# Dense token chunks ranked one by one beside the gate stage, with TensorE's order written out there

## The chip, the cores and the metric

One core of a Trainium2 chip runs the kernel. TensorE (PE; its weight loads are PEld), VectorE (DVE), ScalarE (ACT), GpSimd (POOL) and SyncE (SP, which here issues most transfers) work side by side, each through its own list in order, and wait for each other by semaphores. The metric is the device time of one execution in microseconds; the median of three runs of the kernel before is 1878.28 us (1877.82 to 1882.6).

## What is computed

One layer of a decoder on 512 prompt tokens and 64 sample tokens. Two branches (a short convolution, and attention over a window of 128 with sinks) are merged by sigmoid gates, normed, and followed by a product-key expert layer, which takes most of the time:

```python
qv = einsum('nd,de->ne', xb, w_pq)                      # 8 heads, two halves of 128
s = einsum('nhpc,hpkc->nhpk', qv, sub_keys)             # 128 keys in each half
top_s, top_i = lax.top_k(s, 16)                         # the 16 best of each half
best_s, sel = lax.top_k(sums_of_pairs(top_s), 16)       # the 16 best pairs = experts
gate = softmax(best_s)
pre = einsum('nd,nhkd->nhk', xb, expert_u[idx])         # 16384 experts
out = einsum('nhk,nhkd->nd', gate * gelu(pre), expert_v[idx])
y = layer_norm(alpha * h + out)
```

`sums_of_pairs` stands here for the sums of the two halves' best keys, with the expert's number beside each.

## The kernel before

**Waves and chunks.** Tokens go through in two waves. The first wave holds chunk 0 and the sample chunk; their experts' rows are gathered one by one (an indirect DMA on GpSimd, a multiply-and-sum on VectorE: tile `junk`, line 525). The second wave holds the dense chunks 1, 2 and 3 (128, 128 and 64 tokens; the sixty-four rows beside chunk 3 come from the first wave). For these all 16384 experts are computed, in 128 tables of 128 experts, and a gate matrix with zeros picks the chosen ones.

**Float32 by halves.** A matrix product of float32 numbers is three matmuls: each operand is split into a high part (`whi`, on ScalarE, line 119) and the rest (`wlo`, on GpSimd or VectorE, line 120), and `mm3` (lines 123 to 125) adds three of the four products.

**The second wave's stages.**
- Projections, convolution, and attention, which needs the mask `mask_p`, the keys `kT_all` and the values `v_all`.
- The merge of the convolution branch (`merge_conv`): eight times a gate product of 24 matmuls and a convolution product of 12, multiplied on VectorE into the tile `br` (line 661). The convolution products lie in one of three PSUM banks, which `br`'s multiply frees. The merge of the attention branch follows, then the output projection, the norm and the transposes.
- Key scores (`scores`): sixteen weight tables, four per call. After each call VectorE ranks each chunk's 4 heads' halves (`top16`, five instructions for a list of 128) and, when a group of heads has both halves, `route` forms and ranks the pairs and turns them into key numbers.
- First products (`front`): table t of `expert_u` times the tokens, 24 matmuls of 384 columns, GELU, result to DRAM (`spill`) for the first 60 tables and kept for 9 more: 69 (`AHEAD`) in all before the second product begins.
- The gate stage (`gate_matrix`): per four tokens one VectorE comparison makes two one-hot matrices (`hot`, line 785), ScalarE and GpSimd scale one of them by the gate weights, four matmuls (eight instructions in the trace) multiply them, ScalarE or VectorE copies the result into `gb`, and every sixteen tokens `gb` goes to DRAM (`gd`). Three `hot` buffers and three PSUM banks serve it.
- The second product: for each of 128 tables, GELU times gate (`gm`, read back from `gd`), split, 18 matmuls into six banks (`acc`, line 937), and, from the 61st table on, one more first product beside it.

**What sets the order.** The program is recorded in the order of the code; a scheduler that simulates a timeline then puts each engine's instructions in order, and `issue_after` pins one behind another. Gathers of the first wave are woven in as `side` work, one to two after each table. In the code before, five first products follow each call of `scores`, all three chunks are ranked there, and during the gate stage first products are released by a proportion, ten (`KEEP`) being held back and pinned behind the last gate matmul:

```python
for k, g4 in enumerate((0, 2, 1, 3)):
    scores(second, g4)
    fronts(FQ * (k + 1))
...
for i in range(len(DENSE)):
    for g in gate_matrix(i, *second.sel[i], gd):
        fronts(base + (AHEAD - KEEP - base) * (i * (128 // GN) + g + 1) // total)
with tc.issue_after(newest[1]):
    fronts(AHEAD)
```

Of the kernel before, what the change touches and what calls it, by code (L numbers as in the profile page):

```python
# [17 lines left out]
AF = mybir.ActivationFunctionType  # L18
# [41 lines left out]


ORDER = "qkscscasacsca"
FQ = 5
KEEP = 10
LAST = 2


# [8 lines left out]
def step_kernel(ctx: ExitStack, tc: tile.TileContext, I: dict, O: dict):  # L76
# [28 lines left out]
    loads, newest = [], [None, None]  # L105

    def late(dst, src):

# [13 lines left out]
    def mm3(ps, L, R, start, stop):  # L122
        PE.matmul(ps, L[0], R[0], start=start, stop=False)  # L123
        PE.matmul(ps, L[0], R[1], start=False, stop=False)  # L124
        PE.matmul(ps, L[1], R[0], start=False, stop=stop)  # L125

    def in_order(calls):
        last = None
# [22 lines left out]
    side_work = []  # L151

    def side(n):
        while n > 0 and side_work:
            try:
                next(side_work[0])
                n -= 1
            except StopIteration:
                side_work.pop(0)
# [261 lines left out]
    def route(val, pos, sel, hs):  # L421
# [36 lines left out]
        for k, (s1, s2, off) in enumerate((((4, ALU.logical_shift_right), (2, ALU.logical_shift_right), -12.0),  # L458
                                           ((15, ALU.bitwise_and), (3, ALU.bitwise_and), 0.0))):
            u1 = f128("u1", U32)  # L460
            u2 = f128("u2", U32)
            V.tensor_single_scalar(u1, bp, s1[0], op=s1[1])
            V.tensor_single_scalar(u2, bp, s2[0], op=s2[1])
            rk = f128("rk")
            V.scalar_tensor_tensor(rk, u2, off, u1, op0=ALU.add, op1=ALU.subtract)
            V.tensor_tensor(rk, rk, mk, op=ALU.mult)
            V.tensor_tensor(rk, rk, u1, op=ALU.add)
            oh = tmp("k", [128, 4, 16, 16], "oh", dt=BF16)[:r]
            V.tensor_tensor(oh.rearrange("p h k a -> p (h k) a"), rk.unsqueeze(2).broadcast_to([r, 64, 16]),
                            numbers[0][:r, :16].unsqueeze(1).broadcast_to([r, 64, 16]), op=ALU.is_equal)  # L470
            V.tensor_tensor(oh, oh, pf[:, :, k, :].unsqueeze(2).broadcast_to([r, 4, 16, 16]), op=ALU.mult)
            V.tensor_reduce(keys[k], oh.rearrange("p h k a -> p (h k) a"), axis=AX.X, op=ALU.add)

    def key_tiles():
        return [tmp("k", [128, 128], f"kk{k}", bufs=3) for k in range(2)]
# [187 lines left out]
    def merge_attention(s):  # L663
# [59 lines left out]
        if s.w == 0:  # L723
# [4 lines left out]
        s.sel = [sel3 if c == 3 else (key_tiles(), gate[c] if c in GATHER else tmp("k", [128, 128], "gt", bufs=2))  # L728
                 for c in s.chunks]

    def scores(s, g4):

        sk = tmp("w", [128, 512], "raw", name="sk", bufs=RAW["w"])
        S.dma_start(sk, I["sub_keys"][g4])
        low = g4 < 2
        pss = []
        for i, r in enumerate(s.rows):
            if r == 128:
                pss.append(bank("mm"))
            else:  # L740

                if low:
                    s.half = bank("mm")
                pss.append(s.half[:64] if low else s.half[64:128])
        for j in range(4):
            ps = product(s, weight(s, I["w_pq"][g4 * 4 + j]), s.hT, 8, "u")
            qv = tmp("k", [128, s.mv], "qv", bufs=2)
            A.activation(qv, ps, AF.Copy)
            for i, r in enumerate(s.rows):
                where = dict(tile_position=(0, 64)) if r == 64 and not low else {}  # L750
                PE.matmul(pss[i][:, j * 128:(j + 1) * 128], qv[:, i * 128:i * 128 + r],
                          sk[:, j * 128:(j + 1) * 128], start=True, stop=True, **where)
        for i, r in enumerate(s.rows):
            if r == 64 and low:
                continue
# [3 lines left out]
            for j in range(4):  # L759
                top16(s.val[i][:, g * 4 + j, :], s.pos[i][:, g * 4 + j, :], sc[:, j, :], 128)  # L760
            if r == 64 and g == 1:
                keys, gt = s.sel[i]
                kh, gh = [tmp("k", [128, 64], f"kh{k}") for k in range(2)], tmp("k", [128, 64], "gh")
                route(s.val[i], s.pos[i], (kh, gh), 0)
                for dst, src in zip((*keys, gt), (*kh, gh)):
                    A.activation(dst[:64, :64], src[:64], AF.Copy)
                    S.dma_start(dst[:64, 64:128], src[64:128])
            elif r == 128 and g4 % 2:
                route(s.val[i], s.pos[i], s.sel[i], g4 // 2)


    def gate_matrix(i, keys, gt, gd):
# [3 lines left out]
        iota_ps = pt[:, 384:512]  # L776
        T = tmp("k", [128, 3, 128], "T3")
        A.activation(T, pt[:, :384].rearrange("p (k n) -> p k n", k=3), AF.Copy)
        for g in range(128 // GN):
            gb = tmp("b", [128, 128, GN], "gb", bufs=2)  # L780
            for q in range(GN // 4):
# [5 lines left out]
                for r in range(4):  # L787
                    oi = hot[:, 0, r, :]
                    weight_of = T[:, 2, n + r:n + r + 1]
                    if GATED[r] == "a":  # L790
                        A.activation(oi, oi, AF.Copy, scale=weight_of)  # L791
                    else:
                        G.tensor_scalar(oi, oi, weight_of, None, op0=ALU.mult)
                    newest[1] = PE.matmul(ps[:, r * 128:(r + 1) * 128], hot[:, 1, r, :], oi, start=True, stop=True).ins  # L794
# [6 lines left out]
            S.dma_start(gd[i * (128 // GN) + g], gb)  # L801
            yield g


    spill = dram.tile([NS, 128, ND], F32, name="spill")
# [2 lines left out]
    ks, bs = ExitStack(), ExitStack()  # L808
    pools["k"] = ks.enter_context(pool("k", "left"))
    pools["mm"] = ks.enter_context(psum("mm", 3))  # L810
    at_stack = ExitStack()
    pools["at"] = at_stack.enter_context(psum("at", 3))
    sel3 = ([tmp("k", [128, 128], f"k3{k}") for k in range(2)], tmp("k", [128, 128], "gt3"))
# [36 lines left out]
    hT = second.hT  # L850
    coef = {}

    def front(t):
        wu = table(I["euT"][t], "w", G if t < AHEAD else V, PACE_U[t % len(PACE_U)] if t < AHEAD else 0)
        ps = bank("u")
        for k in range(8):
            mm3(ps[:, :ND], block(wu, k), (hT[0][:, k, :], hT[1][:, k, :]), k == 0, k == 7)
# [9 lines left out]
    done = 0  # L867

    def fronts(n):
        nonlocal done  # L870
        while done < min(n, NE):
            front(done)
            done += 1

    for k, g4 in enumerate((0, 2, 1, 3)):
        scores(second, g4)
        fronts(FQ * (k + 1))
    total = len(DENSE) * 128 // GN
    base = done
    for i in range(len(DENSE)):  # L880
        for g in gate_matrix(i, *second.sel[i], gd):
            fronts(base + (AHEAD - KEEP - base) * (i * (128 // GN) + g + 1) // total)
    with tc.issue_after(newest[1]):
        fronts(AHEAD)
    bs.close()
    ks.close()
    del pools["hp"]
# [39 lines left out]
        return calls  # L927

    for t in range(NE + 1):
        fronts(t + LAG)  # L930
        if t < NE:
            middle(t)
        if 1 <= t <= NE - LAST:
# [115 lines left out]
```

## Time and profile before

| | us |
|---|---|
| median of the runs | 1878.28 |
| profiled execution, its own time | 1882.06 |
| its span | 1880.3 |
| TensorE busy | 1733.5 (92%) |
| VectorE busy | 1507.2 (80%) |
| GpSimd busy | 1111.2 (59%) |
| ScalarE busy | 782.1 (42%) |
| DMA, mean rate | 264 GB/s |

Times in rows count from the span's start. A busy TensorE is not TensorE at its peak: its matmuls overlap, so what counts is the distance from one start to the next. PEclk is the granted clock: 1.00 is its higher level (2.4 GHz), 0.5 its lower (1.2 GHz), and a value between is a mix of both over the stretch. An engine's idle time costs only where another waits for it. In the page's chain that ended last TensorE holds 49%, VectorE 24%, transfers 10%.

### The profile page before, as it was taken

To read this page: it belongs to the slowest core of one execution; us is meant where nothing else is said; L and a number is where in the kernel's file an instruction comes from. 1 tells how busy PE (TensorE), PEld (TensorE's weight loads), DVE (VectorE), ACT (ScalarE), POOL (GpSimd) and SP (SyncE) were. 2 spreads that over 40 slices of the span, in tenths; PEclk is the share of its full clock that TensorE was granted. 3 is DMA by queue.
4 is the path that set the end of the run, shared out by engine and by line. 5 is a ranking of instruction groups with operands and counts; after the bars stand their busy time and mean duration, and the time that the engine had idled before them with its cause. 6 is when DMAs were issued, how large, how long until landed. Compare 5 with 4: busy or idle time off the path is not lost.

```text
span 1880.3 us, 27617 instructions
## 1 busy us (share of the span) xinstructions
PE 1733.5 (92%) x9760; PEld 1573.5 (84%) x9760; DVE 1507.2 (80%) x2632; ACT 782.1 (42%) x1339; POOL 1111.2 (59%) x724
## 2 busy tenths in 40 slices
PE   7999998897989998699979899999999999999985
PEld 7997798887779888699978777787899999998974
DVE  6646689998955699998896677878778888888897
ACT  4554343442333433367785333333333333343322
POOL 4445433466756667688835522223578777778883
PEclk9999999997989999799999899999999999999998
DMA  7445443357757678799947999999989999989973
GB/s 246 156 134 213 130 135 118 113 186 254 277 192 249 232 239 276 248 326 363 338 187 253 330 327 328 345 336 341 322 311 353 335 327 353 350 299 339 326 264 108
DMA packets 190539, 496.50 MB, mean 264 GB/s; under 512 B 17712, under 2 KB 83696, under 8 KB 187312
## 3 DMA queue, kind: packets, MB, share of 16 engines
q1 hardware_dynamic: 135104, 293.39, 45.5%
q0 software_dynamic: 55296, 201.35, 30.1%
q8 instruction: 76, 1.25, 0.3%
q14 instruction: 63, 0.52, 0.1%
HBM read 454.48 MB, written 40.54 MB: 263 GB/s over the span
## 4 chain that ended last, share of the span: by engine, by line
PE 49%; DVE 24%; DMA 10%; issue 7%; POOL 5%; ACT 5%; SPq 1%; DVEq 0%; POOLq 0%; ACTq 0%
PE acc L937 19%; PE ps L123 9%; PE ps L124 8%; PE ps L125 8%; POOL wlo L120 3%; DMA re<-spill 3%; DVE junk L525 3%; PE ps L794 2%; POOL g L511 2%; DVE wlo L120 2%; DMA raw<-in_euT 2%; ACT whi L119 1%; ACT hot L791 1%; DMA g<-in_eu,idx 1%; DVE s L415 1%
## 5 line engine op out<-in xcount | busy, mean ns | idle before, releaser
L120 POOL TENSOR_TENSOR wlo<-raw,whi 128x1024 fp32r<-128x1024 f32 x232 | 580.0, 2503 | 320.6 <-ACT whi L119 287.9
L119 ACT ACTIVATE whi<-raw 128x1024 fp32r<-128x1024 f32 x388 | 409.2, 1056 | 590.0 <-PE ps L124 235.9
L123 PE MATMUL ps<-xhi,whi 128*128 128x384 f32 (+2 forms) x1600 | 531.3, 332 | 34.3 <-ACT sp L860 27.8
L125 PE MATMUL ps<-xhi,wlo 128*128 128x384 f32 (+2 forms) x1600 | 527.4, 330 | 1.6 <-POOL wlo L120 1.6
L124 PE MATMUL ps<-xlo,whi 128*128 128x384 f32 (+2 forms) x1600 | 527.6, 330 | 0.0
L534 DVE SCALAR_TENSOR_TENSOR h<-g,pre,h 128x1024 f32<-128x1024 f32 x192 | 316.2, 1647 | 71.7 <-DMA g<-in_ev,idx 70.4
L511 POOL DMA_INDIRECT g<-in_eu,idx x192 | 206.6, 1076 | 241.3 <-DVE junk L525 186.5
L123 PEld LDWEIGHTS ps<-xhi,whi 128*128 128x128 f32 x1600 | 309.6, 194 | 44.3 <-ACT sp L860 30.3
L511 POOL DMA_INDIRECT g<-in_ev,idx x192 | 255.0, 1328 | 126.5 <-DVE h L534 87.3
L124 PEld LDWEIGHTS ps<-xlo,whi 128*128 128x128 f32 x1600 | 309.3, 193 | 3.6 <-issue 0.9
L125 PEld LDWEIGHTS ps<-xhi,wlo 128*128 128x128 f32 x1600 | 308.6, 193 | 3.0 <-POOL wlo L120 2.1
L937 PE MATMUL acc<-whi,chi 128*128 128x512 f32 x756 | 292.4, 393 | 14.7 <-ACT chi L119 8.4
L937 PE MATMUL acc<-wlo,chi 128*128 128x512 f32 x756 | 299.6, 396 | 5.7 <-POOL wlo L120 5.7
L937 PE MATMUL acc<-whi,clo 128*128 128x512 f32 x756 | 258.1, 394 | 2.1 <-DVE clo L120 2.1
L120 DVE TENSOR_TENSOR wlo<-raw,whi 128x1024 fp32r<-128x1024 f32 x156 | 204.6, 1312 | 49.1 <-ACT whi L119 48.9
L937 PEld LDWEIGHTS acc<-whi,chi 128*128 128x128 f32 x756 | 143.1, 189 | 47.1 <-ACT chi L119 11.7
L937 PEld LDWEIGHTS acc<-wlo,chi 128*128 128x128 f32 x756 | 144.1, 191 | 37.0 <-POOL wlo L120 8.2
L525 DVE SCALAR_TENSOR_TENSOR junk<-g,hp 128x1024 bf16<-128x1024 f32 x104 | 125.7, 1209 | 56.9 <-DMA g<-in_eu,idx 54.8
L937 PEld LDWEIGHTS acc<-whi,clo 128*128 128x128 f32 x756 | 143.6, 190 | 32.8 <-DVE clo L120 2.7
L785 DVE TENSOR_TENSOR hot<-pt,T 128x1024 f32<-128x1024 f32 x96 | 114.0, 1217 | 17.1 <-PE ps L794 12.1
L525 DVE SCALAR_TENSOR_TENSOR junk<-g,h 128x1024 bf16<-128x1024 f32 x88 | 123.7, 1406 | 3.1 <-DMA g<-in_eu,idx 2.8
L794 PE MATMUL ps<-hot 128*128 128x128 f32 x768 | 111.6, 289 | 15.2 <-ACT hot L791 14.0
(252 smaller groups left out, 2205.5 us busy)
## 6 DMA issues: line engine op xcount, KB each, us to landing
raw<-in_euT SPq DMA_DIRECT2D x128, 512.0 KB, 6.1
raw<-in_ev SPq DMA_DIRECT2D x128, 512.0 KB, 5.0
gd<-gb SPq DMA_DIRECT2D x24, 1024.0 KB, 5.2
gm<-gd SPq DMA_DIRECT2D x48, 512.0 KB, 9.7
raw<-in_w_g SPq DMA_DIRECT2D x32, 512.0 KB, 3.4
raw<-in_w_pq SPq DMA_DIRECT2D x32, 512.0 KB, 4.2
raw<-in_w_bch SPq DMA_DIRECT2D x24, 512.0 KB, 3.5
spill<-sp SPq DMA_DIRECT2D x60, 192.0 KB, 4.2
```

Source lines behind the costliest of these rows:

```text
L119: A.activation(hi, src, AF.Copy)
L120: return (eng or V).tensor_tensor(lo, src, hi.bitcast(F32), op=ALU.subtract)
L123: PE.matmul(ps, L[0], R[0], start=start, stop=False)
L124: PE.matmul(ps, L[0], R[1], start=False, stop=False)
L125: PE.matmul(ps, L[1], R[0], start=False, stop=stop)
L415: V.match_replace(s2, val[:, 0:8], s, -3.0e38)
L511: G.indirect_dma_start(out=rows[i], out_offset=None, in_=I[src], in_offset=bass.IndirectOffsetOnAxis(ap=idx[c][:, s:s + 1], axis=0))
L525: V.scalar_tensor_tensor(junk, g, 1.0, in_psum(c), op0=ALU.mult, op1=ALU.mult, accum_out=p)
L534: V.scalar_tensor_tensor(h_tok[c], g, p, h_tok[c], op0=ALU.mult, op1=ALU.add)
L785: V.tensor_tensor(hot, iota_ps.unsqueeze(1).unsqueeze(1).broadcast_to([128, 2, 4, 128]), T[:, 0:2, n:n + 4].unsqueeze(3).broadcast_to([128 ...
L794: newest[1] = PE.matmul(ps[:, r * 128:(r + 1) * 128], hot[:, 1, r, :], oi, start=True, stop=True).ins
L937: PE.matmul(*args, **kw)
```

## The change

**Ranking.** `rank` becomes a generator that can stop after each list and inside `route`. In the second wave only the first dense chunk (chunk 1) is ranked in `scores` itself. For chunks 2 and 3 the scores stay in tiles of their own (`sc10` to `sc21`), and their ranking is recorded step by step in the gate loop: chunk 2's 34 steps beside chunk 1's gates, chunk 3's 17 beside chunk 2's.

**First products in eighths.** `front` yields after every three matmuls. Four instead of five first products follow each call of `scores`. In the gate loop each four tokens are followed by 5, 4 or 3 eighths, by chunk, and `issue_after(order[0])` chains gate matmuls and eighths in just this order on TensorE. Five first products remain for the time after the gates. The next table's load is recorded in the middle of a first product.

**Memory.** `mask_p`, `kT_all` and `v_all` leave the lasting constants for a pool `kv` that is closed after the second wave's attention. The tile `br` of the second wave, which is taken later from the same side, covers part of its space.

```diff
-FQ = 5
-KEEP = 10
+FQ = 4
+STEPS = (5, 4, 3)
+RANKS = (34, 17, 0)
...
-    mask_p = const("mask_p", [128, 256], src=I["mask_p"])
...
-    kT_all = const("kT_all", [128, SEQ])
-    v_all = const("v_all", [128, 5, 128])
...
+    def rank(s, i, g, sc):
+
+        for j in range(4):
+            top16(s.val[i][:, g * 4 + j, :], s.pos[i][:, g * 4 + j, :], sc[:, j, :], 128)
+            yield
...
+        elif s.rows[i] == 128 and g % 2:
+            yield from route(s.val[i], s.pos[i], s.sel[i], g // 2)
...
+    def run(steps, n=10 ** 6):
+        while n > 0 and steps:
+            try:
+                next(steps[0])
+                n -= 1
+            except StopIteration:
+                steps.pop(0)
...
-            sc = tmp("kb"[s.w], [128, 4, 128], "sc", bufs=2 + s.w * 2)
+            sc = tmp(*(("b", [128, 4, 128], f"sc{i}{g}") if s.w and i else ("k", [128, 4, 128], "sc", "sc", 2)))
             A.activation(sc, src.rearrange("p (j n) -> p j n", j=4), AF.Copy)
...
+            if s.w and i:
+                ranking.setdefault(i, []).append(rank(s, i, g, sc))
+            else:
+                run([rank(s, i, g, sc)])
...
+                with tc.issue_after(order[0]):
+                    for r in range(4):
...
+                        mm = PE.matmul(ps[:, r * 128:(r + 1) * 128], hot[:, 1, r, :], oi, start=True, stop=True)
+                order[0] = mm.ins
...
+    kvs = ExitStack()
+    pools["kv"] = kvs.enter_context(pool("kv", "left"))
+    mask_p, kT_all = tmp("kv", [128, 256], "mask_p"), tmp("kv", [128, SEQ], "kT_all")
+    v_all = tmp("kv", [128, 5, 128], "v_all")
...
     first.rs.close()
+    kvs.close()
...
+            if base <= t < AHEAD:
+                with tc.issue_after(order[0]):
+                    order[0] = mm3(*args).ins
+            else:
+                order[0] = mm3(*args).ins
+            if k == 3 and base <= t < AHEAD - 1:
+                load_u(t + 1)
+            if k < 7:
+                yield
...
+    T = gate_columns(*second.sel[0])
     for i in range(len(DENSE)):
-        for g in gate_matrix(i, *second.sel[i], gd):
-            fronts(base + (AHEAD - KEEP - base) * (i * (128 // GN) + g + 1) // total)
-    with tc.issue_after(newest[1]):
-        fronts(AHEAD)
+        left = ranking.get(i + 1, [])
+        nxt = None
+        for q, _ in enumerate(gate_matrix(i, T, gd)):
+            run(todo, STEPS[i])
+            fronts.done += STEPS[i]
+            run(left, (q + 1) * RANKS[i] // 28 - q * RANKS[i] // 28)
+            if q == 28:
+                run(left)
+                if i + 1 < len(DENSE):
+                    nxt = gate_columns(*second.sel[i + 1])
+        T = nxt
+    fronts(AHEAD)
```

**Where instructions move.** First VectorE's list around the end of the second wave's last attention, before the change: `o` is that attention's output, `br` the merge of the convolution branch, `junk` a gather of the first wave.

```order
L252 TENSOR_REDUCE pmx<-t_4153 64x4
L661 TENSOR_TENSOR br<-bg,ps 128x320
L525 SCALAR_TENSOR_TENSOR junk,pre<-g,h_94 128x1024
...
L264 RECIPROCAL prd<-pden 64x4
L525 SCALAR_TENSOR_TENSOR junk,pre<-g,h_94 128x1024
L311 TENSOR_TENSOR o<-ps,prd 64x4x64
L120 TENSOR_TENSOR alo<-ps,ahi 128x4x64
```

The `br` shown is the last of eight; all eight stand ahead of `o`. The same place in the changed kernel:

```order
L304 TENSOR_TENSOR o<-ps,prd 64x4x64
L658 TENSOR_TENSOR br<-cg,ps 128x320
L658 TENSOR_TENSOR br<-bg,ps 128x320
L658 TENSOR_TENSOR br<-cg,ps 128x320
L121 TENSOR_TENSOR alo<-ps,ahi 128x4x64
L658 TENSOR_TENSOR br<-bg,ps 128x320
L658 TENSOR_TENSOR br<-cg,ps 128x320
L522 SCALAR_TENSOR_TENSOR junk,pre<-g,h_91 128x1024
L658 TENSOR_TENSOR br<-bg,ps 128x320
```

All eight now stand behind `o`; on TensorE five of the eight convolution products have moved behind that attention's transposes with them.

Next, TensorE's list at the end of the gate stage before the change; line 794 is a gate matmul, lines 123 to 125 a first product, `pt` the transposed key numbers of the last chunk.

```order
L123 MATMUL ps<-xhi,whi 128x384
L124 MATMUL ps<-xlo,whi 128x384
L125 MATMUL ps<-xhi,wlo 128x384
L794 MATMUL ps<-hot 128x128 x76
L775 MATMUL pt<-ident,k_111 128x128
L775 MATMUL pt<-ident,k_112 128x128
L775 MATMUL pt<-ident,gt_113 128x128
L794 MATMUL ps<-hot 128x128 x132
```

208 of the 384 gate matmuls stand there without a first product between them. The end of the same stage in the changed kernel (gate matmuls at line 815, first products at 124 to 126):

```order
L815 MATMUL ps<-hot 128x128 x4
L124 MATMUL ps<-xhi,whi 128x384
L125 MATMUL ps<-xlo,whi 128x384
L126 MATMUL ps<-xhi,wlo 128x384
L124 MATMUL ps<-xhi,whi 128x384
L125 MATMUL ps<-xlo,whi 128x384
L126 MATMUL ps<-xhi,wlo 128x384
L124 MATMUL ps<-xhi,whi 128x384
L125 MATMUL ps<-xlo,whi 128x384
L126 MATMUL ps<-xhi,wlo 128x384
L815 MATMUL ps<-hot 128x128 x4
```

Each four gate matmuls are now followed by three eighths here, and by five and four in the two chunks before.

Last, VectorE's list where the changed kernel's gate stage begins: `hot` is a gate's one-hot pair, `MAX`, `MAX_INDEX` and `MATCH_REPLACE` are ranking.

```order
L409 MAX val_5473<-s_7398 128x8
L410 MAX_INDEX pos_5476<-val_5473,s_7349 128x8
L805 TENSOR_TENSOR hot<-pt,T_6987 128x1024 x3
L410 MAX_INDEX pos_5476<-val_5473,s_7398 128x8
L408 MATCH_REPLACE s_7435<-val_5473,sc_6420 128x128
L408 MATCH_REPLACE s_7441<-val_5473,sc_6420 128x128
L805 TENSOR_TENSOR hot<-pt,T_6987 128x1024
L409 MAX val_5473<-s_7435 128x8
```

Before the change no ranking of a dense chunk stood behind the first `hot`; now the second chunk's stands between its rows.

## Rows read from the trace of the kernel before

**Rows 1.** Stage windows: stretch, length, busy of PE, PEld, DVE, ACT, POOL; clock, DMA.
```profile
420.00:437.00 17.00, 6.07 (x29) 3.98 (x30) 14.87 (x24) 5.03 (x14) 10.90 (x8) 0.57 0.72 243
437.00:537.00 100.00, 86.16 (x453) 74.60 (x454) 88.22 (x105) 34.09 (x50) 65.80 (x35) 0.89 0.67 236
537.00:686.00 149.00, 141.12 (x849) 134.31 (x849) 95.06 (x381) 55.43 (x79) 104.48 (x62) 0.99 0.72 241
686.00:811.00 125.00, 103.83 (x550) 102.52 (x550) 124.88 (x335) 42.67 (x60) 84.94 (x55) 0.88 0.80 259
811.00:932.00 121.00, 121.00 (x824) 121.00 (x823) 99.36 (x124) 88.98 (x211) 107.20 (x99) 1.00 0.96 350
932.00:1010.00 78.00, 62.81 (x422) 56.06 (x421) 70.11 (x73) 67.21 (x195) 34.16 (x53) 0.96 0.51 206
1010.00:1062.00 52.00, 43.01 (x233) 42.37 (x231) 22.31 (x22) 17.49 (x24) 30.05 (x18) 0.92 0.94 321
1062.00:1285.00 223.00, 214.83 (x921) 175.24 (x922) 172.52 (x261) 76.10 (x101) 57.64 (x55) 0.98 0.97 335
```
**Rows 2.** Timeline of ScalarE: start, duration, line, operation.
```profile
672.04 0.42 ACT L748 ACTIVATE qv<-ps 128x320 f32<-128x320 f32 x1
...
932.09 0.47 ACT L860 ACTIVATE sp<-ps 128x384 f32<-128x384 f32 x1
...
1057.03 0.49 ACT L864 ACTIVATE gel<-ps 128x384 f32<-128x384 f32 x1 [3.67 <-PE ps L125]
```
**Rows 3.** Gate tile: ns least, median, most; first and last start.
```profile
L794 PE MATMUL ps<-hot x768: 270/275/582, 813.5 to 1008.4; 128*128 128x128 f32 x192
```
**Rows 4.** Second product's banks, the same columns.
```profile
L937 PE MATMUL acc<-whi,chi x756: 387/389/767, 1062.4 to 1852.2; 128*128 128x512 f32 x189
```
**Rows 5.** Timeline of VectorE in the second wave's last attention.
```profile
382.06 0.21 DVE L466 TENSOR_TENSOR rk<-rk,mk 128x64 f32<-128x64 f32 x1
...
386.36 1.21 DVE L120 TENSOR_TENSOR wlo<-raw,whi 128x1024 fp32r<-128x1024 f32 x1
...
418.44 0.47 DVE L661 TENSOR_TENSOR br<-bg,ps 128x320 f32<-128x320 f32 x1
...
435.11 0.42 DVE L311 TENSOR_TENSOR o<-ps,prd 64x256 f32<-64x256 f32 x1 [0.84 <-PE ps L134]
```
**Rows 6.** Timeline of TensorE: matmuls of three widths.
```profile
391.08 0.31 PE L123 MATMUL ps<-xhi,whi 128*128 128x320 f32 x1
...
391.52 0.31 PE L123 MATMUL ps<-xhi,whi 128*128 128x320 f32 x1
...
689.17 0.33 PE L123 MATMUL ps<-xhi,whi 128*128 128x384 f32 x1
...
689.69 0.33 PE L123 MATMUL ps<-xhi,whi 128*128 128x384 f32 x1
...
860.36 1.72 PE L794 MATMUL ps<-hot 128*128 128x128 f32 x14
```
**Rows 7.** Gathers (tile junk) in one window, VectorE busy.
```profile
537.00:811.00 274.00, 70.08 (x115) 0.94 0.75 250
```
**Rows 8.** Lists of ranking (tile val) in the same window, VectorE busy.
```profile
537.00:811.00 274.00, 58.85 (x330) 0.94 0.75 250
```
**Rows 9.** Groups by line: count, busy, mean ns of one, idle before.
```profile
L466 DVE TENSOR_TENSOR rk<-rk,mk 128x64 f32<-128x64 f32 x18 | 18.6, 1036 | 0.0
...
L785 DVE TENSOR_TENSOR hot<-pt,T 128x1024 f32<-128x1024 f32 x96 | 114.0, 1217 | 17.1 <-PE ps L794 12.1 <-ACT T L778 2.1 <-ACT hot L791 1.3
...
L800 DVE COPY gb<-ps 128x512 f32<-128x512 f32 x24 | 16.4, 685 | 9.6 <-PE ps L794 9.6
```
**Rows 10.** DMA issues: count, KB each, median us to landing.
```profile
gd<-gb SPq DMA_DIRECT2D x24, 1024.0 KB, 5.2
gm<-gd SPq DMA_DIRECT2D x48, 512.0 KB, 9.7
```
**Rows 11.** Gate tile in one window: busy of PE, PEld, DVE, ACT, POOL.
```profile
932.00:1010.00 78.00, 61.31 (x410) 54.29 (x408) 57.49 (x49) 47.77 (x150) 29.77 (x50) 0.96 0.51 206
```

More of the change, by code (lines that the diff above doesn't have):

```diff
@@ L103, in tmp @@
         return pools[p].tile(shape, dt, tag=tag, name=name or tag, bufs=bufs)
-    loads, newest = [], [None, None]
+    loads, newest, order = [], [None], [None]
     def late(dst, src):
@@ L124, in mm3 @@
         PE.matmul(ps, L[0], R[1], start=False, stop=False)
-        PE.matmul(ps, L[1], R[0], start=False, stop=stop)
+        return PE.matmul(ps, L[1], R[0], start=False, stop=stop)
     def in_order(calls):
@@ L153, in side @@
     def side(n):
[L154 to L159, printed above, removed]
+        run(side_work, n)
     ident = const("ident", [128, 128])
     make_identity(nc, ident)
-    mask_p = const("mask_p", [128, 256], src=I["mask_p"])
     convw = const("convw", [128, 4, 3], src=I["conv_w"])
@@ L729, in merge_attention @@
                  for c in s.chunks]
+    ranking = {}
+    def rank(s, i, g, sc):
+        for j in range(4):
+            top16(s.val[i][:, g * 4 + j, :], s.pos[i][:, g * 4 + j, :], sc[:, j, :], 128)
+            yield
+        if s.rows[i] == 64 and g == 1:
+            keys, gt = s.sel[i]
+            kh, gh = [tmp("k", [128, 64], f"kh{k}") for k in range(2)], tmp("k", [128, 64], "gh")
+            yield from route(s.val[i], s.pos[i], (kh, gh), 0)
+            for dst, src in zip((*keys, gt), (*kh, gh)):
+                A.activation(dst[:64, :64], src[:64], AF.Copy)
+                S.dma_start(dst[:64, 64:128], src[64:128])
+        elif s.rows[i] == 128 and g % 2:
[7 more added lines that the diff above has]
+                steps.pop(0)
     def scores(s, g4):
@@ L756, in scores, with gate_columns @@
             src, g = (pss[i], g4) if r == 128 else (s.half, g4 - 2)
-            sc = tmp("kb"[s.w], [128, 4, 128], "sc", bufs=2 + s.w * 2)
+            sc = tmp(*(("b", [128, 4, 128], f"sc{i}{g}") if s.w and i else ("k", [128, 4, 128], "sc", "sc", 2)))
             A.activation(sc, src.rearrange("p (j n) -> p j n", j=4), AF.Copy)
[L759 to L772, printed above, removed]
+            if s.w and i:
+                ranking.setdefault(i, []).append(rank(s, i, g, sc))
+            else:
+                run([rank(s, i, g, sc)])
+    def gate_columns(keys, gt):
         pt = shared[0]
@@ L775, in gate_matrix @@
             PE.transpose(pt[:, k * 128:(k + 1) * 128], src, ident)
-        iota_ps = pt[:, 384:512]
-        T = tmp("k", [128, 3, 128], "T3")
+        T = tmp("k", [128, 3, 128], "T3", bufs=2)
         A.activation(T, pt[:, :384].rearrange("p (k n) -> p k n", k=3), AF.Copy)
+        return T
+    def gate_matrix(i, T, gd):
+        iota_ps = shared[0][:, 384:512]
         for g in range(128 // GN):
@@ L786, in gate_matrix @@
                                 T[:, 0:2, n:n + 4].unsqueeze(3).broadcast_to([128, 2, 4, 128]), op=ALU.is_equal)
[L787 to L794, printed above, removed]
+                with tc.issue_after(order[0]):
+                    for r in range(4):
+                        oi = hot[:, 0, r, :]
+                        weight_of = T[:, 2, n + r:n + r + 1]
+                        if GATED[r] == "a":
+                            A.activation(oi, oi, AF.Copy, scale=weight_of)
+                        else:
+                            G.tensor_scalar(oi, oi, weight_of, None, op0=ALU.mult)
+                        mm = PE.matmul(ps[:, r * 128:(r + 1) * 128], hot[:, 1, r, :], oi, start=True, stop=True)
+                order[0] = mm.ins
                 dst = gb[:, :, q * 4:(q + 1) * 4]
@@ L800, in gate_matrix @@
                     V.tensor_copy(dst, src)
-            S.dma_start(gd[i * (128 // GN) + g], gb)
-            yield g
+                if q == GN // 4 - 1:
+                    S.dma_start(gd[i * (128 // GN) + g], gb)
+                yield
     spill = dram.tile([NS, 128, ND], F32, name="spill")
@@ L810, in step_kernel @@
     pools["mm"] = ks.enter_context(psum("mm", 3))
+    kvs = ExitStack()
+    pools["kv"] = kvs.enter_context(pool("kv", "left"))
+    mask_p, kT_all = tmp("kv", [128, 256], "mask_p"), tmp("kv", [128, SEQ], "kT_all")
+    v_all = tmp("kv", [128, 5, 128], "v_all")
+    loads.insert(0, (mask_p, I["mask_p"]))
     at_stack = ExitStack()
@@ L851, in step_kernel, with load_u @@
     coef = {}
+    ready = {}
+    def load_u(t):
+        if t not in ready and t < NE:
+            ready[t] = table(I["euT"][t], "w", G if t < AHEAD else V, PACE_U[t % len(PACE_U)] if t < AHEAD else 0)
     def front(t):
-        wu = table(I["euT"][t], "w", G if t < AHEAD else V, PACE_U[t % len(PACE_U)] if t < AHEAD else 0)
+        load_u(t)
+        wu = ready.pop(t)
         ps = bank("u")
         for k in range(8):
-            mm3(ps[:, :ND], block(wu, k), (hT[0][:, k, :], hT[1][:, k, :]), k == 0, k == 7)
+            args = (ps[:, :ND], block(wu, k), (hT[0][:, k, :], hT[1][:, k, :]), k == 0, k == 7)
+            if base <= t < AHEAD:
+                with tc.issue_after(order[0]):
+                    order[0] = mm3(*args).ins
+            else:
+                order[0] = mm3(*args).ins
+            if k == 3 and base <= t < AHEAD - 1:
+                load_u(t + 1)
+            if k < 7:
+                yield
         if t < NS:
@@ L865, in front @@
             coef[t] = ge
-    done = 0
+        yield
+    base = 4 * FQ
+    todo = [front(t) for t in range(NE)]
     def fronts(n):
[L870 to L873, printed above, removed]
+        run(todo, 8 * n - fronts.done)
+        fronts.done = max(fronts.done, 8 * n)
+    fronts.done = 0
     for k, g4 in enumerate((0, 2, 1, 3)):
@@ L929, in step_kernel @@
     for t in range(NE + 1):
-        fronts(t + LAG)
+        fronts(min(t + LAG, NE))
         if t < NE:
```

4 lines of the change are left out of this document (2 added, 2 removed).

## The prediction

> **What bounds the kernel now.** I read the stage windows first, since the whole-run shares (TensorE 92%, VectorE 80%) mix stages that have different limits. The reader is to see in [rows 1] that the bottleneck changes hands. From 437 to 686 us TensorE is nearly full (86.16 of 100, then 141.12 of 149). From 686 to 811 VectorE is full (124.88 of 125) with ranking and gathers, while TensorE idles 21 us. From 811 to 932 TensorE is full and VectorE has 22 us left. From 932 to 1010 no engine is full: gates stand there without first products beside them. Until 1062 transfers run at 0.94, and after that TensorE again is full. Then the timelines for the marks: the last score projection lands at 672.04 and the 59th first product at 932.09 [rows 2], gates run from 813.5 to 1008.4 [rows 3], the second product begins at 1062.4 [rows 4]. What follows 1062 is not touched, so the question is how these marks move. The profiled execution takes 1882.06 us, 3.8 over the median of the runs; I sum against it and take 3.8 off at the end.
>
> **A, the merge falls behind the attention.** The new pool lets `br` lie where the mask, keys and values of attention lay, so `br`'s first write waits until the second wave's attention is done. Before, all eight `br` were written by 418.44, ahead of `o` at 435.11 [rows 5]; now all stand behind `o`. TensorE's convolution products share three banks that `br` frees, so five of them (60 matmuls) and the six gate products behind them (144) fall behind `o` too. At 0.147 us a matmul of 320 columns (three in 0.44, [rows 6]) that is 30.0 us. TensorE idled ahead of `o` already (6.07 busy of 17, [rows 1]) and now idles longer. VectorE's list up to `o` is shorter by seven `br` (0.47), two splits (1.21 each, [rows 5]) and a gather (1.22 with its second record: 70.08 us for 115 records, two each, [rows 7]): 6.9 us, so `o` comes at about 428. Of the 23 left, the idle 13.8 us of 437 to 537 take back two or so: **+21**. Bounds: 10, if most of that idle time is filled; 30, if `o` doesn't come earlier.
>
> **B, fewer first products ahead of the last scores.** Three calls of four instead of five: three fewer. One is eight times 0.52 us [rows 6], 4.16. **-12.5**: the last projection lands at 672 + 21 - 12.5, about 681.
>
> **C, the wait for the first gate.** All VectorE time from 537 to 811 less gathers is 95.06 + 124.88 - 70.08, about 150 us [rows 1, 7]. The 40 lists of 128 take 58.85, or 1.47 each [rows 8]; the other 91 are five `route` passes of 18.2. A chunk of 128 tokens has 16 lists and two passes: 60 us; the 64-token chunk 30. After the last scores VectorE still has four lists and a pass for chunk 1 (24.1), by the order the first two steps of eight deferred lists (4.7) and about 34 instructions of chunk 2 pulled ahead (9.7), and nine gathers (11.0): 49.5. The first `hot` comes at 731, the first gate matmul at 733, where it was 813.5. Only three or so first products stand there for TensorE, so it idles some 38 us. Its clock will drop (0.57 over the 17 us in which it was busy for 6, [rows 1]), but VectorE sets the pace.
>
> **D, the gate stage.** Per four tokens TensorE has eight gate records (14 in 1.72, so 0.98 us, [rows 6]) and 5, 4 or 3 eighths of 0.52.
> - Chunk 1: TensorE 20 products x 4.16 + 32 x 0.98 = 114.6. VectorE: 32 `hot` of 1.217 and 7 copies of 0.685 [rows 9] = 43.7, 25 gathers = 30.5, ranking 57 (90 for chunks 2 and 3, less 14 of first steps that the order puts ahead of the gates, 9.7 of C, and 9 left to chunk 2's gates): **131**. VectorE decides.
> - Chunk 2: TensorE 16 x 4.16 + 31.4 = **98**; VectorE 43.7 + 30.5 + 9, about 83.
> - Chunk 3: 12 x 4.16 + 31.4 = **81.3**.
>
> Together 310, where it was 195 with fewer first products beside it; the last gate ends at 1043.5, before at 1008.4.
>
> `hot` has three buffers and the gates three banks, so a gate matmul that waits is not rare; behind it now queue its eighths, behind these GELU and spill on ScalarE and SP. VectorE has slack for that in chunks 2 and 3; in chunk 1 it is the bound anyway.
>
> One price is open. The multiply of line 466 takes 0.21 us once at 382.06 [rows 5], but 1036 ns on average [rows 9]; GpSimd is busy 84.94 of 125 us in the stretch in which the kernel before ranks, and 107.20 of 121 beside its gates [rows 1]. I keep the measured means.
>
> The Trainium skill, "SBUF — State Buffer", section "SBUF: two separate sides", says that VectorE and GpSimd share a port pair, held as an exclusive lock against a GpSimd read while VectorE reads two SBUF operands. The rows of line 466 agree in kind. By that rule ranking beside gates would be a few us dearer, an estimate of 4 from the two busy shares, and the sum +15.
>
> **E, the end of the stage.** Behind the last gate five first products and three eighths: 22.4 us, to 1066. Before, the last GELU at 1057.03 [rows 2] preceded the second product at 1062.4 [rows 4] by 5.4; the same gap gives 1071.3. **+9** against 1062.4.
>
> **F, transfers.** From the last gate the way to the second product is `gd` 5.2, `gm` 9.7 [rows 10] and a split, about 18 us: just hidden by the 22.4. Before, 52 us at 0.94 [rows 1], 49 us of transfers, lay there. Now 28 lie there, and five fewer first products (five tables and the seven or so gathers beside them, each 1024 x 128 float32 or 0.52 MB, about 6.4 MB at 335 GB/s, [rows 1]) save 19; the remaining 30 us stand against 28, hence **+2**. Bounds: 0 (hidden), 19 (nothing saved).
>
> **At nothing:** the second buffer of the transposed key numbers, the generators, and the next table's load in mid-product (the same 69 loads; if one came late TensorE would wait for part of a 4.16). SP's queue carries the same transfers; the mask's load moves only in its list.
>
> **Sum.** +9 +2 = +11: 1893 against the profiled execution, **1889** against the median. Seen as a whole: ranking beside gates fills GpSimd's and TensorE's time, but VectorE stays the bound until chunk 2, and A costs more than B saves.
>
> **Rivals.**
> 1. *Faster, 1860.* VectorE in chunk 1 is not the bound: ranking fits in the 22 us that it has free beside the gates of 811 to 932 [rows 1], so chunk 1 goes at TensorE's 114.6 (-16), and half of A is filled (-11): about -29 against the forecast. For it: the gate stage of before left TensorE 15 idle us and 49 of 78 for `hot` alone [rows 1, 11]. Against: 131 is a sum of measured times. Its chance rests on the rows above alone. The Trainium skill, "Perfetto Trace Analysis", section "Optimization Strategy", says that where the most-contended engine changes over time, interleaving the regimes may improve performance; by that, this rival would hold.
> 2. *The same, 1878.* A costs 10: free time of 437 to 537 takes it, the rest as forecast, -11.
> 3. *Slower, 1929.* The fixed order makes each gate wait for its `hot` with nothing else allowed past. Alone, four tokens take 78 / 49 = 1.59 us [rows 11]; with eighths in series of 2.6, 2.08 and 1.56 the chunks take 134, 117.5 and 100.8: 352 instead of 310, +40. Against: three buffers run ahead. It decides from the point where `hot`, its scaling and its copy take longer than 0.98 plus the eighths, which is chunk 3 first.
> 4. *The change does not do what it says*, if the order were broken up; the order rows show that it holds, so no chance of its own.
>
> **How the numbers follow.** Forecast (slower, 1884 to 1915) 0.52, rival 1 0.20, rival 2 0.16, rival 3 0.12. A measurement of this kernel tells about 0.3% from no change, 5.6 us: 1872.6 to 1883.9 is the same. So faster 0.20, same 0.16, slower 0.64. Range: low, A at 10, chunk 1 at 114.6 and F at 0, about 1860; high, A at 30, VectorE 10% dearer in chunk 1 and F at 19, about 1928. I cut both ends a little: 1864 to 1920, which leaves about 2 in 10 out: some half of rival 1 and most of rival 3.
>
> **What would show it.** `o` at about 428 with all `br` behind it, and the second wave's scores later by some 20 less the first products skipped; the first `hot` near 731 after a TensorE wait at its lower level of 1.2 GHz; VectorE full through chunk 1 and TensorE through chunks 2 and 3; the last gate near 1044 and the second product near 1071. Wrong: the first gate before 715, or chunk 1's gates in under 120 us (rival 1); chunk 3's gates in over 95 (rival 3); a wait of over 8 us between the last GELU and the second product (F).

## The result and the profile after

The changed kernel is slower: 1905.99 us median against 1878.05 of the kernel before, ratio 1.0151 (95% interval 1.0127 to 1.0175); run again beside the experiments, 1.0151 (1.0124 to 1.0178). Forecast was 1889. The sign was right and the time lies in the range, but +28 is two and a half times the forecast +11. The profiled executions took 1882.06 and 1903.54, 21.5 apart; the rest is that the one of before lay 4.0 above its median and that of after 2.4 below its own.

The marks of the changed kernel come from its tile views (least, median, most ns; first and last start), and answer to [rows 2 to 5]:

```profile
L304 DVE TENSOR_TENSOR o<-ps,prd x10: 398/409/425, 56.4 to 417.6; 128x256 f32<-128x256 f32 x8, 64x256 f32<-64x256 f32 x2
...
L658 DVE TENSOR_TENSOR br<-bg,ps x4: 471/484/489, 418.3 to 447.0; 128x320 f32<-128x320 f32 x4
...
L770 ACT ACTIVATE qv<-ps x32: 361/399/437, 220.2 to 673.8; 128x256 f32<-128x256 f32 x16, 128x320 f32<-128x320 f32 x16
...
L815 PE MATMUL ps<-hot x768: 269/275/583, 722.3 to 1053.5; 128*128 128x128 f32 x192
...
L991 PE MATMUL acc<-whi,chi x756: 386/390/794, 1078.8 to 1873.9; 128*128 128x512 f32 x189
```

The gate chunks below are cut at the 1st, 257th and 513th gate record.

| us | before | forecast | after |
|---|---|---|---|
| `o` of the second wave's attention | 435.1 | 428 | 417.6 |
| last score projection | 672.0 | 681 | 673.8 |
| first gate matmul | 813.5 | 733 | 722.3 |
| chunk 1's gates | 87 | 131 | 131.5 |
| chunk 2's gates | 65 | 98 | **120.2** |
| chunk 3's gates | 42 | 81.3 | 79.4 |
| last gate matmul | 1008.4 | 1043.5 | 1053.5 |
| second product begins | 1062.4 | 1071.3 | 1078.8 |
| from there to the end of the span | 817.9 | 819.9 | 822.9 |

One number is far out, chunk 2 (the last row of the table holds the forecast's F, +2). The stage windows of after (stretch, length, busy of PE, PEld, DVE, ACT, POOL; clock, DMA), which answer to [rows 1], are the wait for the first gate, the three chunks, and the end of the stage:

```profile
674.00:722.30 48.30, 16.89 (x93) 15.21 (x91) 43.52 (x182) 11.32 (x18) 19.88 (x14) 0.71 0.54 190
722.30:853.80 131.50, 120.12 (x740) 118.55 (x741) 127.85 (x327) 82.16 (x177) 94.36 (x81) 0.94 0.77 268
853.80:974.00 120.20, 104.30 (x644) 102.26 (x644) 77.84 (x97) 64.51 (x154) 81.47 (x72) 0.93 0.75 272
974.00:1053.40 79.40, 78.13 (x535) 77.75 (x535) 59.50 (x73) 58.35 (x141) 63.38 (x60) 1.00 0.89 322
1053.40:1078.70 25.30, 22.72 (x132) 22.40 (x131) 7.91 (x12) 6.28 (x10) 11.32 (x9) 1.00 0.98 342
```

Chunk 1 is as forecast: VectorE is busy 127.85 of 131.5 us. In chunk 2 no engine is full. TensorE idles 16 us and its clock is 0.93, though VectorE has only 78 us of work. What VectorE waits for (total us, times, longest), first after, in chunk 2, then before, in its whole gate stage from 811 to 1010:

```profile
DVE junk L522 <- DMA g<-in_eu,idx: 35.5, 8, 6.9
```
```profile
DVE junk L525 <- DMA g<-in_eu,idx: 1.9, 3, 0.8
```

So VectorE stands before gathers. Its timeline in chunk 2, then GpSimd's (start, duration, line, operation; in brackets the idle time before and what ended it):

```profile
878.95 1.22 DVE L805 TENSOR_TENSOR hot<-pt,T 128x1024 f32<-128x1024 f32 x1
886.07 1.22 DVE L522 SCALAR_TENSOR_TENSOR junk<-g,hp 128x1024 bf16<-128x1024 f32 x1 [5.90 <-DMA g<-in_eu,idx]
887.22 0.08 DVE L522 DVE_READ_ACCUMULATOR junk<-g,hp 128x1 f32 x1
887.22 2.35 DVE L805 TENSOR_TENSOR hot<-pt,T 128x1024 f32<-128x1024 f32 x2
...
893.50 1.22 DVE L805 TENSOR_TENSOR hot<-pt,T 128x1024 f32<-128x1024 f32 x1
901.23 1.22 DVE L522 SCALAR_TENSOR_TENSOR junk<-g,hp 128x1024 bf16<-128x1024 f32 x1 [6.52 <-DMA g<-in_eu,idx]
```
```profile
888.53 0.60 POOL L814 TENSOR_SCALAR hot<-hot,T 128x128 f32<-128x128 f32 x1 [3.54 <-DVE hot L805]
890.50 2.40 POOL L121 TENSOR_TENSOR wlo<-raw,whi 128x1024 fp32r<-128x1024 f32 x1 [1.36 <-ACT whi L120]
893.05 1.02 POOL L508 DMA_INDIRECT g<-in_eu,idx  x1
894.37 0.94 POOL L508 DMA_INDIRECT g<-in_eu,idx  x1 [0.30 <-issue]
```

The reader is to see a closed round. VectorE is free at 894.7, but next in its list is a `junk` that starts when its gather lands, at 901.23. By its semaphore this is the gather that GpSimd issued at 893.05, 8.2 us before; the issue stood behind a split (890.50), the split behind a scaling (888.53), and the scaling waited for a `hot` that stood behind the `junk` of 886.07. From 886.07 to 901.23 one round takes 15.2 us and carries four `hot`; TensorE needs 12 for these (rows at 3.0). The price on TensorE, from here to the end of the chunk:

```profile
896.02 0.80 PE L815 MATMUL ps<-hot 128*128 128x128 f32 x2 [2.16 <-POOL hot L814]
...
911.17 0.49 PE L815 MATMUL ps<-hot 128*128 128x128 f32 x2 [1.39 <-POOL hot L814]
...
926.72 0.80 PE L815 MATMUL ps<-hot 128*128 128x128 f32 x2 [2.15 <-POOL hot L814]
...
962.64 2.08 PE L815 MATMUL ps<-hot 128*128 128x128 f32 x8 [7.90 <-ACT hot L812]
968.02 1.05 PE L815 MATMUL ps<-hot 128*128 128x128 f32 x8
971.02 1.05 PE L815 MATMUL ps<-hot 128*128 128x128 f32 x8
```

About every 15 us a gate waits. The longest wait lies ahead of chunk 2's last three `hot`, which stand behind two gathers' uses; the second gather was issued at 950.18 and used at 959.78 (GpSimd, then VectorE):

```profile
950.18 1.01 POOL L508 DMA_INDIRECT g<-in_eu,idx  x1
```
```profile
959.78 1.22 DVE L522 SCALAR_TENSOR_TENSOR junk<-g,hp 128x1024 bf16<-128x1024 f32 x1 [6.77 <-DMA g<-in_eu,idx]
960.93 3.48 DVE L805 TENSOR_TENSOR hot<-pt,T 128x1024 f32<-128x1024 f32 x3
```

After it the row runs at the lower level of 1.2 GHz (granted clock 0.50 from 962.6 to 964.8): eight records take 2.08 us, where the next take 1.05. So each row of four tokens takes 3.0 us but for seven, which together are 24 us longer: about half of it in the rounds, 12.4 at this one wait and the slow row behind it.

### The profile page after: what moved, and what is told of

Read it like the earlier page. It is cut to its first block, busy times and chain, and to the rows that moved or that the text cites. A ratio compares the mean times of both kernels' runs of the same rounds, so it can differ in the third digit from the quotient of the medians.

```text
span 1901.7 us, 27592 instructions
## 1 busy us (share of the span) xinstructions
PE 1728.3 (91%) x9760; PEld 1570.0 (83%) x9760; DVE 1471.3 (77%) x2632; ACT 778.7 (41%) x1335; POOL 1112.7 (59%) x724
## 4 chain that ended last, share of the span: by engine, by line
PE 41%; DVE 14%; DMA 11%; issue 6%; POOL 4%; ACT 2%; SPq 0%; DVEq 0%; ACTq 0%; POOLq 0%
PE acc L991 17%; PE ps L124 7%; PE ps L126 7%; PE ps L125 7%; DMA g<-in_eu,idx 3%; PE ps L815 3%; POOL wlo L121 3%; DMA g<-in_ev,idx 2%; DVE junk L522 2%; DMA raw<-in_ev 2%; DMA re<-spill 2%; DVE wlo L121 2%; POOL g L508 1%; DVE hot L805 1%; DMA raw<-in_w_pq 1%
## 5 line engine op out<-in xcount | busy, mean ns | idle before, releaser
L531 DVE SCALAR_TENSOR_TENSOR h<-g,pre,h 128x1024 f32<-128x1024 f32 x192 | 311.4, 1622 | 75.1 <-DMA g<-in_ev,idx 70.2
L508 POOL DMA_INDIRECT g<-in_ev,idx x192 | 261.3, 1361 | 126.6 <-DVE h L531 78.9
L991 PE MATMUL acc<-whi,clo 128*128 128x512 f32 x756 | 253.2, 395 | 1.1 <-DVE clo L121 1.1
L815 PEld LDWEIGHTS ps<-hot 128*128 128x128 f32 x768 | 103.6, 197 | 31.3 <-ACT hot L812 20.5
```

What stands on the lines that cost most here:

```text
L508: G.indirect_dma_start(out=rows[i], out_offset=None, in_=I[src], in_offset=bass.IndirectOffsetOnAxis(ap=idx[c][:, s:s + 1], axis=0))
L531: V.scalar_tensor_tensor(h_tok[c], g, p, h_tok[c], op0=ALU.mult, op1=ALU.add)
L815: mm = PE.matmul(ps[:, r * 128:(r + 1) * 128], hot[:, 1, r, :], oi, start=True, stop=True)
L991: PE.matmul(*args, **kw)
```

## The experiments

Ratios are to the kernel before, timed on the same chip. Of the changed kernel run again (1.0151) it was said:

> The changed kernel once more, unedited, so that the others of this call have it beside them. Every theory expects 1.0127 to 1.0175 of the kernel before, some 1906 us, with chunk 2's gates taking 120 us and VectorE waiting 40 to 50 us for gathers in the gate stage.

Its chunk 2 took 124.2 us, and VectorE waited 52.8 us for gathers in the gate stage, a little over the 50 (48.8 in the first profile).

**Fetched three ahead** (1.0112, 1.0083 to 1.0141; the changed kernel again 1.0151).

```diff
-GLAG = 2
+GLAG = 3
```


> Gathers are fetched three ahead instead of two (still four buffers). Theory: in chunk 2 VectorE stands 6 to 7 us in every 15 for a gather that was issued only one table before; behind it stands a hot, behind that GpSimd's scaling, the next split and the next gather issue, a closed round of 15 us for 16 eighths that TensorE needs 12 for. With one more fetched ahead these waits fall from 48.8 us to under 15, chunk 2 from 120 to about 100, chunk 1 stays near 124 (VectorE full), and the time is 15 to 20 us under the changed kernel, about 1888. Rival 1 (the fixed order itself makes TensorE wait for hot, its scaling and the copies): the gate stage keeps its 331 us, time within 5 of the changed kernel. Rival 2 (transfers bound the end): the gate stage shortens by 15 to 20 but the wait behind it and the second product lengthen by as much, time within 5.

Chunk 2 took 120.0 us, its waits for gathers 34.9, and the gate stage 334: near rival 1, and my theory's number failed. But the edit had not done what I meant. The uses on VectorE are pinned to nothing, and each moved a step forward with its data. Counted in the order of the trace, 1 to 5 rows of `hot` lie between a gather's fetch on GpSimd and its use on VectorE in chunk 2, with two or three ahead alike (mean 3.75; 6.25 in chunk 2 of the kernel before). This count sorts the waits of the changed kernel: of the nine uses three rows or fewer behind their fetch eight waited, of the fifteen at four or five rows none. The run leaves the question open; its 7 us under the changed kernel lie within the two intervals.

**The gather's use behind the gates** (0.9987, 0.9970 to 1.0004; median 1876.4).

```diff
-GLAG = 2
+GLAG = 3
...
+                hots[0] = V.tensor_tensor(hot, ...).ins
...
+                with tc.issue_after(hots[0]) if hots[0] else ExitStack():
+                    V.scalar_tensor_tensor(junk, g, 1.0, in_psum(c), ...)
```


> Each junk (the gather's use on VectorE) is pinned behind the newest hot recorded, with gathers fetched three ahead, so in VectorE's list of chunk 2 a gather's use stands 5 to 6 rows of four tokens behind its fetch in GpSimd's list, where in the changed kernel it is 3 to 5 (in the run with three fetched ahead and no pin it stayed 3 to 5, which is why that run could not tell). Theory (chunk 2 goes at the round of gather, hot, scaling, split, next gather): waits of VectorE for gathers in chunk 2 fall to a third or less, chunk 2 from 120 to 98 to 104, chunk 1 within 5 of 131.5, time 13 to 20 under the changed kernel (ratio to before about 1.005 to 1.008). Rival 1 (the fixed order makes TensorE wait): chunk 2 stays within 5 of 120. Rival 2 (transfers bound the end): chunk 2 falls, the second product comes no earlier, time within 5 of the changed kernel.

With 4 to 6 rows between fetch and use (mean 5.25) VectorE no longer waits for a gather in chunk 2. Its three chunks:

```profile
709.50:848.40 138.90, 122.35 (x740) 120.87 (x741) 138.88 (x333) 80.97 (x175) 99.07 (x85) 0.91 0.77 267
848.40:948.90 100.50, 98.16 (x645) 97.89 (x644) 81.95 (x104) 65.53 (x157) 82.72 (x74) 0.98 0.91 327
948.90:1026.60 77.70, 77.70 (x537) 77.70 (x535) 61.92 (x76) 58.12 (x141) 64.88 (x60) 1.00 0.93 335
```

Chunk 2 takes 100.5 us with the order on TensorE still fixed: my theory, and neither rival. More came than expected, 1.6% (the difference of the two ratios), some 30 us: the first gate also comes 13 us earlier (two gathers' uses stand in the wait for it instead of ten) and chunk 1 gives back 7 of that. Chunk 1 was 2.4 us further off than its bound of 5.

**No gather in the gates.** The 69 gathers come later, and the whole time (1996.9, one run) is not to be read.

```diff
-PACE_U[t % len(PACE_U)] if t < AHEAD else 0
+PACE_U[t % len(PACE_U)] if t < base else 0
```


> No gather is woven into the gate stage; its 69 gathers come later, so the whole time says nothing. Theory: chunk 2 goes at TensorE's sum, 98 to 102, chunk 1 at 115 to 118 (VectorE has 30 us less: 101 of work), chunk 3 about 80. Rival 1 (fixed order): chunk 2 stays within 5 of 120.

```profile
708.20:829.10 120.90, 118.19 (x739) 117.92 (x740) 95.46 (x273) 81.73 (x177) 67.17 (x54) 0.95 0.49 174
829.10:928.20 99.10, 96.76 (x645) 96.48 (x645) 52.70 (x49) 64.63 (x154) 57.75 (x48) 1.00 0.57 199
```

Chunk 2 at 99.1 agrees with TensorE's sum of 98. Chunk 1 came out 3 us over what I expected; VectorE is no longer its bound (95.46 of 120.9).

**Five eighths in chunk 2** (1.0130, 1.0086 to 1.0175).

```diff
-STEPS = (5, 4, 3)
+STEPS = (4, 5, 3)
```


> STEPS (4, 5, 3) instead of (5, 4, 3): chunk 2's gates get five eighths behind each four tokens, chunk 1's four; all else as changed. Theory (in chunk 2 the gather round sets the pace, not TensorE's work): the 16.6 us of first products added to chunk 2 are nearly free, it takes 120 to 127 (as chunk 1 did with five eighths in the run that ranked all first, 122.6); chunk 1, which VectorE's work sets, loses five gathers, 124 to 131; time within 8 of the changed kernel. Rival (TensorE's sum plus fixed waits of 22 us): chunk 2 at 135 to 139, chunk 1 at 114 to 118.

```profile
716.70:842.00 125.30, 109.55 (x643) 106.08 (x644) 121.92 (x315) 75.36 (x167) 79.11 (x71) 0.91 0.65 232
842.00:966.50 124.50, 116.37 (x741) 115.34 (x740) 88.55 (x109) 71.81 (x165) 97.03 (x83) 0.97 0.85 312
```

Four more first products, 16.6 us of TensorE's work, lengthen chunk 2 by 4.3, as expected; they lie in its idle time, and VectorE's waits for gathers fall to 19.8 us. So TensorE's work did not set the 120. Chunk 1 stays with VectorE.

**All chunks ranked first** (1.0298, 1.0264 to 1.0332, two runs).

```diff
-            if s.w and i:
-                ranking.setdefault(i, []).append(rank(s, i, g, sc))
-            else:
-                run([rank(s, i, g, sc)])
+            run([rank(s, i, g, sc)])
```


> All three chunks are ranked ahead of the gates as in the kernel before, with the eighths and their order as changed. Theory: the first gate comes some 60 us later (the ranking of chunks 2 and 3 left beside the gates, 57 + 9, in front of it), chunk 1 loses its ranking but keeps its gathers, whose round of 15 us for four rows sets it at 118 to 124 instead of 131.5; chunk 2 stays near 120; time 40 to 55 over the changed kernel. Rival (VectorE alone sets chunk 1 and no gather round exists): chunk 1 at 115, time 35 to 40 over.

The first gate came 40 us later, not 60, and the time rose by some 28 (1.0298 against 1.0151): I had charged the ranking too much. Chunk 1 took 122.6, within my 118 to 124 and not the rival's 115, with 21.6 us of waits for gathers, and chunk 2 121.8 with 45. Within the new order, ranking beside the gates is worth these 28 us; it is not the loss.

**The memory pool alone** (1.0090, 1.0058 to 1.0123), the kernel before with nothing but the new pool, and **the pool kept** (1.0073, 1.0045 to 1.0101), the changed kernel with `br` out of its space:

```diff
     first.rs.close()
-    kvs.close()
...
     merge_attention(second)
+    kvs.close()
```


> The kernel before with nothing but the new pool for mask, keys and values (A alone). Theory: 14 us slower than before, last projection at about 686 instead of 672. Forecast's A: 21 slower. Rival (free time of TensorE takes it): within 4 of before.

> The pool of mask, keys and values is closed only after the second wave's merge, so br no longer lies in its space; all else as changed. Theory: A is real and worth what the marks give, last projection at 673.8 against 672.0 in spite of 12.5 us of first products fewer, so 14: the last projection comes at about 660 and the time falls by 10 to 14 against the changed kernel. Forecast's A: 21. Rival (VectorE's ranking of chunk 1, not the projections, sets the first gate): the projection comes earlier, the first gate stays at 722, time within 4.

The last projection with the pool alone, then with the pool kept:

```profile
L745 ACT ACTIVATE qv<-ps x32: 357/400/437, 220.4 to 681.3; 128x256 f32<-128x256 f32 x16, 128x320 f32<-128x320 f32 x16
```
```profile
L770 ACT ACTIVATE qv<-ps x32: 361/400/437, 218.3 to 662.3; 128x256 f32<-128x256 f32 x16, 128x320 f32<-128x320 f32 x16
```

The first gate of the latter comes at 707.3 us, 15 earlier, so what A takes does reach the gates, against the rival of that run; but the three chunks take 4.0, 1.4 and 3.7 us longer, and the second product begins 5.3 earlier. By the projection A costs 9.2 us in the one and 11.5 in the other; by the ratios 17 and 15, with intervals of some 6 us on either side. My 14 was too much by the mark, the forecast's 21 still more; by the times neither is out. With the pool alone the second product begins 10.1 us later than before (1072.5), and the rest of the 20 us by which its profiled execution is longer lies behind that (827.8 us instead of 817.9), where nothing was changed.

**TensorE's order free** (0.9945, 0.9923 to 0.9968; median 1868.46).

```diff
-                with tc.issue_after(order[0]):
-                    order[0] = mm3(*args).ins
+            mm3(*args)
...
-                with tc.issue_after(order[0]):
                     for r in range(4):
```


> TensorE's order isn't fixed: no chaining of gate matmuls and eighths, all else as changed. Theory: the time stays within 10 of the changed kernel, since VectorE's list (gathers before hot) is what the gates wait for, in any order of TensorE. Rival 1 (the fixed order costs the 21 us that the gate stage is longer than forecast): 20 or more faster than the changed kernel.

My expectation failed: by the ratios it is 39 us under the changed kernel. The wait for the first gate, and chunk 2:

```profile
673.70:737.10 63.40, 58.20 (x317) 56.69 (x316) 59.33 (x203) 24.45 (x37) 47.46 (x32) 0.95 0.87 297
...
874.10:974.00 99.90, 99.17 (x656) 98.21 (x655) 89.62 (x114) 69.89 (x164) 83.59 (x75) 1.00 0.91 330
```

TensorE works 58 of 63 us ahead of the first gate, where the fixed order lets it work 17 of 48: eight more first products by then (24 against 16), for a first gate 15 us later. And chunk 2 has no gather round (3.9 us of waits). So two things at least come back at once, and three last runs are to take them apart: gathers' uses behind the gates with the pool kept, order fixed (0.9956, 0.9938 to 0.9973); order free with the pool kept (**0.9886**, 0.9859 to 0.9912; median 1856.9); and all three edits (0.9950, 0.9932 to 0.9967).

> Gathers' uses behind the gates (three fetched ahead) and the kv pool closed only after the merge, TensorE's order still fixed. Theory (A and the gather round are two separate costs): their savings of 14.6 and 28 us add up, ratio to before 0.990 to 0.993, some 1864. Rival (the time that A gives back is lost in the wait for the first gate or in chunk 1, where VectorE is full): ratio within 0.003 of the run with the gathers' uses moved alone, 0.9987.

> TensorE's order free and the kv pool closed only after the merge. Theory: A's 14 us come off the 0.9945 of the run with the order free, ratio 0.986 to 0.989. Rival as above: within 0.003 of 0.9945.

> All three: order free, gathers' uses behind the gates, kv pool closed after the merge. Theory (the fixed order costs by the gather round, which either edit removes): within 0.004 of the run with the order free and the pool kept. Rival (the fixed order has a cost of its own beside it): over 0.004 faster than the run with the gathers' uses moved and the pool kept, at the same place of the gathers' uses.

The second met its expectation; the first and the third did not. With the order fixed and the uses behind the gates, keeping the pool saves 0.3% where 0.8% was expected, at the edge of the rival; with the order free it saves 0.6%. With the uses behind the gates the free order gains nothing (0.9950 against 0.9956), so the rival of the third, a cost of the fixed order beside the round, is out at that place of the uses; but the run with the scheduler's own places is 0.0064 better. Why the pinned uses lose to the scheduler's own places under a free order stays open: its last gate comes earlier (1015 against 1024), its second product begins later (1042 against 1039) and takes 826 us against 817. Order free with the pool kept beats both kernels.

## Why the forecast was wrong

**The failed step** is in D: "Chunk 2: TensorE 16 x 4.16 + 31.4 = 98; VectorE about 83", with "VectorE has slack for that in chunks 2 and 3". The two sums were near (TensorE's bare time 99.1 without gathers, VectorE busy 77.84), but the maximum of two sums is the pace only if the lists let each engine run ahead. I priced a gather at its 1.22 us on VectorE. The 35.5 us for which VectorE stood before it, with `hot` behind, were not in the sum. They cost 22 us (16 in which TensorE stood idle, 6 in which it worked longer, at a mean clock of 0.93), twice the forecast's whole +11; without gathers, or with their uses further back, chunk 2 took 99.1 and 100.5. The kernel before would have warned me. VectorE's waits there from 537 to 686 us:

```profile
DVE junk L525 <- DMA g<-in_eu,idx: 52.9, 10, 12.3
```

In that stage VectorE had the time to spare; I took a gather's 1.22 us as all that it can cost.

**A** had the right mechanism, with all `br` behind `o`, and was mis-sized: 21 forecast, 9 to 12 measured at the last projection (15 to 17 by the times). `o` came at 417.6 instead of 428: VectorE had more than the list's own durations to gain. **B** gave 7.5 of its 12.5 (681.3 with the pool alone, 673.8 with both), or 9.7 (672.0 before, 662.3 with the pool kept).

**C** held (48.5 against 51.7), with TensorE nearly idle from 695 us and its clock at 0.50 from there to the first gate. I counted this idle time as free because VectorE sets the pace; the run with the order free filled it with eight products.

**D** for chunks 1 and 3 and **E** held within 3 us. **F**: 5 us instead of 2, but this stretch took 817 to 828 us in runs with an equal code there, so it is not resolved. Its sign of being wrong, over 8 us between the last GELU and the second product, was met by the letter (1068.68 and 1078.75). But TensorE worked for most of that on the last two first products, whose GELUs came later, and stood idle for 2.63 us, where it had been 5.37 before.

Added up against the forecast: -7 to the scores, -3 in the wait, +22 in chunk 2, -2 in chunk 3 and -3 behind the gates, +3 at the end, about +10 in the profiled executions.

**Rivals.** 1 is out: chunk 1 was VectorE's. Its two terms add up to -27, not -29, and the 49 that it reads in [rows 11] is the count of `hot` on VectorE: gate matmuls hold TensorE for 61.31 of those 78 us. 2 is out by the time, though its A of 10 is near what the projections show. 3 named the fixed order, but by the length of `hot`, scaling and copy, and said chunk 3 would show it first; chunk 3 ran at TensorE's sum. That its 117.5 for chunk 2 lies near the 120.2 measured is luck. The pins do matter, since a free TensorE escapes the round, but through gathers that nobody named.

**The open price.** The Trainium skill, "SBUF — State Buffer", section "SBUF: two separate sides", has VectorE's operations on two SBUF inputs and GpSimd's operations that read SBUF shut each other out for a whole instruction. From it I had estimated ranking beside the gates 4 us dearer. In chunk 1, with GpSimd busy 94 of 131.5 us, five multiplies took 201 to 213 ns:

```profile
L461 DVE TENSOR_TENSOR rk<-rk,mk x5: 201/206/213, 737.3 to 838.4; 128x64 f32<-128x64 f32 x5
```

These 4 us did not come, but the trace agrees with the rule. The mean of 1036 ns [rows 9] is made of two kinds: before, eleven of the 18 multiplies took 196 to 224 ns and overlapped no split on GpSimd; each of the other seven, of 1.8 to 3.0 us, overlapped one and ended 0.1 us behind it. No multiply of chunk 1 met a split; one of chunk 2 did (VectorE, then GpSimd):

```profile
935.96 2.08 DVE L461 TENSOR_TENSOR rk<-rk,mk 128x64 f32<-128x64 f32 x1
```
```profile
935.59 2.38 POOL L121 TENSOR_TENSOR wlo<-raw,whi 128x1024 fp32r<-128x1024 f32 x1
```

So the price hangs on whether a split runs at that moment. I had worked it out from GpSimd's busy share.

## What to carry to other kernels

An engine's sum of busy times bounds a stage only if nothing in its list waits. Look in its in-order list for an operation that needs a transfer, count how many steps lie between the transfer's issue and its use, and compare that with the transfer's time. Here a gather took 8.2 us from issue to use and stood in a queue before its issue: three rows of 3.0 us did not cover that, four or five did. A deeper fetch alone does not help where a scheduler then moves the use forward too: pin the use. And memory that one stage gives up is paid for by whoever has to wait for it, here 9 to 12 us at the last projection for the 5.5 kilobytes a partition of mask, keys and values.

## What was not expected of the hardware

Here a wait cost TensorE more than its length: after 7.9 us of idle time the granted clock was 0.50, eight gate records took 2.08 us instead of 1.05, and the row from 962.64 to 968.02 took 5.4 us instead of 3.0. Already the 2.16 us of idle time ahead of 896.02 brought it from 1.00 to 0.50 (896.0 to 897.6 us). The second product's length, 817 to 828 us, moved between runs by as much as the effects sought.
